# A trunk layer with RWKV-7 and attention heads on one core: interleaved output projection, substitution on blocks of 32, and a step of its own for the loads of the inverse's blocks

## The chip, the cores and the metric

The kernel runs on one core of one Trainium2 chip. The metric is the device time of one execution in microseconds, the median of the runs shown. Weights and activations lie in device memory ahead of the run, and all results are written back to it.

## What is computed

One layer over 1024 prompt frames (a new stream) and 64 sample frames (a continued stream) of width 1024, all in fp32. Cut to what matters:

```
mod = silu(c) @ w_ada + b_ada                  # 6 x 1024 per stream
sh1, sc1, gt1, sh2, sc2, gt2 = split(mod, 6)
h = rms_norm(x) * (1 + sc1) + sh1
proj = h @ w_in                                # 1024 -> 3336 columns
# RWKV-7, 8 heads of 64; per frame:
#   sa = S @ -kk ;  S = S * w + sa (kk * a)^T + v k^T ;  y = S @ r
# attention with forget gates, 8 heads of 64:
#   softmax(q k^T / 8 + decay bias, causal) @ v
mix = concat(y_rwkv, y_fox) @ w_out
x = x + gt1 * mix
h2 = rms_norm(x) * (1 + sc2) + sh2
ffn = (silu(h2 @ w_gate) * (h2 @ w_up)) @ w_down   # 2816 wide
y = x + gt2 * ffn
```

The final RWKV states, the last projected row, the attention keys, values and forget logs are outputs too.

## The kernel before

Activations lie with the features on the 128 partitions and the frames along them. The frames are worked in two halves: half 0 has 512 prompt frames, half 1 the other 512 and the 64 sample frames (576). An fp32 product is made of three fp32r products: each operand is split into a high part, made on ACT, and the rest, made on DVE or POOL, and PE adds hi x hi, lo x hi and hi x lo (`mm3`, L290 to 296; `split`, L209 to 216; the flag `pool_lo` chooses between POOL and DVE). A tile scheduler lays out each engine's list of instructions from the program's order and the data dependences; it also decides which of the ready instructions of two steps stands first. All transfers are issued on SP.

The stages in time:

* The modulation, 48 tiles of w_ada. A tile is loaded whole (512 KB), multiplied by the vector of both streams in eight small matmuls (`ada_mm`, L190), copied by ACT to a row, transposed on PE (L198), and reduced and biased on DVE (L200, L201). The first 16 come ahead of everything; the 32 others run as "background", one with each load of w_in.
* A phase for each half, in an order written out by hand (`ORDER`, L35 and L36). A letter is a step, its digit a pair of heads: Z projects r, k and v of a pair; D makes the decay; A the matrices of the chunks; B the chain over the chunks; N the group norm. Q, K, q, k, V project, norm and store the attention's operands, C copies the cache, L, O and S are small. The last pair's chain of a half, B3, is not in the string: it is done in the next stage, for half 0 as the step T3 of half 1's phase, for half 1 beside the attention's first heads.
* Attention of half 0 and of half 1, with the output projection of half 0 between the heads of half 1.
* `x1_sq` and `h2_make`: the second norm and the FFN's operands of half 0; then the output projection of half 1; then the same for half 1.
* The FFN, products of seven block combinations in place of eight (`ffn`, `fast_half`, `fast_prep`). Its unit is an item: w_gate or w_up of a pair of 128-column blocks, first for half 0, then for half 1. A weight item's combinations are made on DVE and ACT one item ahead. The gated result goes to device memory (actscr).
* The down projection: loads of actscr, their split, and PE's products in groups of four of the 22 blocks (`down`, L1244), the residual on DVE (L1248).

The RWKV step A and B need some detail, since most of the change is there. The frames of a half are cut into chunks of 64: 8 in half 0, 9 in half 1. Step A makes for each chunk and each of a pair's two heads the 64 x 64 lower triangle of the products of kk with k's multiples (pA on PE, L464, masked on DVE by `amask`, L466: tile At). The chain needs (I - triangle)^-1. It is found from the inside: the 16 x 16 blocks on the diagonal (four for each head and chunk, two of them a 32-block; 64 in half 0's A, 72 in half 1's, one on each partition) are written to device memory (dm) and read back as one block a partition (mb). They are inverted there by forward substitution on DVE: 15 steps of two instructions, a product into tb (L488) and a sum into wb (L490). The inverses and their transposes go to device memory again (dw, du), with zeros standing around them since the start.

Step B reads them back with eight transfers (gt and inv, 32-blocks), and merges them: 16-blocks to 32 by three sets of small 32 x 32 matmuls (all by the helper at L523: pg1 with a mask product on DVE at L530, pw1 with a sum at L535, pu1 with copies on ACT at L540), then 32-blocks to 64 by two more sets (pgt, pu12). Then it transposes kb and v, and runs the chain: for each chunk pR on PE (L597), a copy R on DVE and on ACT (one head each, L599, L600), pSA (L610), a copy sv on both (L611, L612), pS (L613), and the next state on DVE (L617), while POOL has made the decayed state sd (L604); pY (L608, L618) is the output. Nothing in a chain can run ahead; the matmuls of the projections (named pmm) stand between its matmuls on PE's list.

Of the kernel before, what the change touches and what calls it, by code (L numbers as in the profile page):

```python
# [16 lines left out]
P = 128  # L17
# [17 lines left out]
ORDER = ("Z0 D0 A0 L B0 D1 Z1 Q0 N0 A1 C0 Z2 q0 D2 V0 O A2 K0 k0 B1 K1 Z3 Q1 q1 V1 N1 D3 A3 V2 C1 S k1 Q2 Q3 B2 q2 N2 K2 k2 V3 K3 k3 C2 C3 q3",  # L35
         "T3 Z0 D0 A0 L Z1 K0 D1 U3 B0 A1 D2 Z2 Q0 N0 k0 A2 q0 D3 Q1 B1 K1 q1 Z3 A3 k1 V2 N1 V1 B2 V0 Q2 q2 K3 N2 Q3 q3 K2 k3 k2 V3")  # L36
# [28 lines left out]
class K:  # L65
# [7 lines left out]
    def consts(self):  # L73
# [14 lines left out]
        self.ct = self.cmid.tile([P, KT, 32], F32, name="ct")  # L88
# [23 lines left out]
    def consts2(self):  # L112
# [17 lines left out]
        for h in range(2):  # L130
            am = self.amask[:, h]
            nc.gpsimd.memset(am[64 * h:64 * h + 64, 0:64], -1.0)
            for r in (0, 64):
                nc.gpsimd.affine_select(out=am[r:r + 64, 0:64], in_=am[r:r + 64, 0:64], compare_op=ALU.is_gt,
                                        fill=0.0, base=0, pattern=[[1, 64]], channel_multiplier=-1)
                nc.gpsimd.affine_select(out=am[r:r + 64, 64:128], in_=am[r:r + 64, 64:128], compare_op=ALU.is_ge,
                                        fill=0.0, base=0, pattern=[[1, 64]], channel_multiplier=-1)
# [199 lines left out]
    def rwkv_persist(self):  # L337
# [4 lines left out]
        for t in self.inv:  # L342
# [3 lines left out]
        self.qmask = self.fper.tile([P, 32], F32, name="qmask")  # L346
        nc.vector.tensor_reduce(self.qmask[:, 0:1], self.ident.rearrange("p (q i s) -> p i q s", i=2, s=16)[:, 1],
                                axis=AX.XY, op=ALU.add)
        nc.vector.tensor_copy(self.qmask[:, 1:16], self.qmask[:, 0:1].to_broadcast([P, 15]))
        nc.gpsimd.memset(self.qmask[:, 16:32], 0.0)  # L350
        zero = self.inv[0].rearrange("p c t -> p (c t)")[0:72, 0:512]
        for t in self.dw + self.du:
            nc.sync.dma_start(t.rearrange("g x s t -> (g x s t)").rearrange("(p t) -> p t", p=72), zero)
# [63 lines left out]
    def rwkv_a(self, hf, j, z, d):  # L417
# [21 lines left out]
        nc.vector.tensor_tensor(rk[:, 0:nch, 0:64], ch(kk), pp[:, 0:nch, 0:64], op=ALU.mult)  # L439
# [30 lines left out]
        nb = 2 * ng  # L470
        dm = self.dpool.tile([2, ng, 2, 16, 16], F32, tag="dm", name="dm")
        for h in range(2):
            for x in range(2):
                for i in range(2):
                    o = 32 * x + 16 * i
                    nc.sync.dma_start(dm[i, h * nch:(h + 1) * nch, x].rearrange("g s t -> s g t"),
                                      At[64 * h + o:64 * h + o + 16, 0:nch, 0, h, o:o + 16])
        mb = self.rpool.tile([72, 16, 16], F32, tag="mb", name="mb")
        nc.sync.dma_start(mb[0:2 * nb], dm.rearrange("i g x s t -> (i g x) s t"))
        wb = self.rpool.tile([72, 16, 16], F32, tag="wb", name="wb")  # L480
        tb = self.rpool.tile([72, 64], F32, tag="tb", name="tb")
        nc.gpsimd.memset(wb[0:2 * nb], 0.0)
        nc.gpsimd.affine_select(out=wb[0:2 * nb], in_=wb[0:2 * nb], compare_op=ALU.not_equal, fill=1.0, base=0,
                                pattern=[[-1, 16], [1, 16]], channel_multiplier=0)
        for s in range(15):
            m = 15 - s
            t_ = tb[0:2 * nb, 0:m * (s + 1)].rearrange("p (a b) -> p a b", b=s + 1)
            nc.vector.tensor_tensor(t_, mb[0:2 * nb, s, s + 1:16].unsqueeze(2).to_broadcast([2 * nb, m, s + 1]),  # L488
                                    wb[0:2 * nb, s:s + 1, 0:s + 1].to_broadcast([2 * nb, m, s + 1]), op=ALU.mult)
            nc.vector.tensor_tensor(wb[0:2 * nb, s + 1:16, 0:s + 1], wb[0:2 * nb, s + 1:16, 0:s + 1], t_, op=ALU.add)  # L490
        nc.vector.tensor_copy(mb[0:2 * nb], wb[0:2 * nb].rearrange("p s t -> p t s"))

        dw, du = [t[j % 2] for t in (self.dw, self.du)]
        for i in range(2):
            r, o = slice(i * nb, (i + 1) * nb), slice(16 * i, 16 * i + 16)
            for d, t in ((dw, wb), (du, mb)):
                nc.sync.dma_start(d[0:ng].rearrange("g x s t -> (g x) s t")[:, o, o], t[r])
        return zv, rk, kb, pc, bon, At, dw, du

    def rwkv_b(self, hf, j, st):  # L500
# [6 lines left out]

        inv, gt = self.inv[j % 2], self.gt
        for h in range(2):
            g = slice(h * nch, (h + 1) * nch)  # L510
            for x in range(2):
                r = slice(64 * h + 32 * x, 64 * h + 32 * x + 32)
                nc.sync.dma_start(gt[r, 0:nch], dw[g, x].rearrange("g s t -> s g t"))
                nc.sync.dma_start(inv[r, 0:nch, r], du[g, x].rearrange("g s t -> s g t"))
# [10 lines left out]

        g1 = self.rpool.tile([P, 9, 32], F32, tag="g1", name="g1")
        pg = small("pg1", (0, 1), lambda h, c, r, o: (At[r, c, 0, h, o], gt[r, c]))
        for h in range(2):
            hs = slice(64 * h, 64 * h + 64)
            nc.vector.tensor_tensor(g1[hs, 0:nch], pg[h][hs, 0:nch],  # L530
# [1109 lines left out]
```

## Time and profile before

| | us |
|---|---|
| median of 3 runs | 1759.04 (1754.95 to 1759.44) |
| the profiled execution, its own time | 1761.91 |
| its span in the profile | 1760.2 |
| mean granted TensorE clock | 0.974 of full speed |
| phase of half 0 | about 44 to 400 |
| phase of half 1 | about 400 to 690 |
| chains B0 to B3 of half 0 | 150 to 181, 213 to 246, 300 to 328, 371 to 398 |
| chains of half 1 | 473 to 507, 550 to 584, 626 to 657, 696 to 731 |
| attention, first scores to last | 705.5 to 921 |
| output projection of half 1 | about 951 to 1014 |
| FFN | 1001 to 1490 |
| down projection | 1490 to 1757 |

The times in the profile count from the start of its span. A chain's times are those of its first and last pSA. PE is TensorE's matmuls, PEld its weight loads; an engine's busy time is the union of its instructions. The table was read from the timeline and from single tiles' rows.

### The profile page before, as it was taken

The page shows a single profiled execution, that of the slowest core. Times are in us where ns is not written, and L with a number is a line of the kernel's source. Part 1 is how long each engine was busy: PE and PEld are TensorE (multiplying, and loading weights), DVE is VectorE, ACT ScalarE, POOL GpSimd, SP SyncE. Part 2 cuts the span into 40 slices and gives each one's busy share as a digit, 9 for nine tenths or more (in the row PEclk, how much of TensorE's full clock was granted, in tenths as well). Part 3 has the DMA queues.
Part 4 walks back from the last instruction along what each step waited for, and adds up shares of the span by engine and source line. Part 5 has one row for each costly group of instructions (what it writes and reads, how often), then busy time and mean ns, then how long its engine had stood idle before and what let it go on. Part 6 is the DMA issues. An engine that isn't in the chain of part 4 may idle for free.

```text
span 1760.2 us, 33567 instructions
## 1 busy us (share of the span) xinstructions
PE 1673.6 (95%) x12893; PEld 1454.0 (83%) x12893; DVE 1105.8 (63%) x2518; ACT 728.0 (41%) x1532; POOL 267.6 (15%) x468
## 2 busy tenths in 40 slices
PE   5999999999999998889999779999999999999999
PEld 3676666688888886666888779999999999999998
DVE  6676676757786753777876685556666654444434
ACT  4435454543555344566776363233333222112110
POOL 2102121121222122100212300000000000222221
PEclk9999999999999997889999899999999999999999
DMA  8435356642233336376663302222222224533313
GB/s 314 151 87 157 116 165 195 184 122 71 76 75 92 107 84 167 96 203 166 158 188 128 106 34 83 74 74 74 74 74 78 79 89 134 182 99 93 99 36 120
DMA packets 136143, 207.10 MB, mean 118 GB/s; under 512 B 64687, under 2 KB 72911, under 8 KB 135983
## 3 DMA queue, kind: packets, MB, share of 16 engines
q1 hardware_dynamic: 135982, 204.95, 39.1%
q8 instruction: 102, 1.67, 0.4%
q14 instruction: 59, 0.48, 0.1%
HBM read 157.65 MB, written 47.25 MB: 116 GB/s over the span
## 4 chain that ended last, share of the span: by engine, by line
PE 81%; DVE 7%; ACT 6%; issue 3%; DMA 3%; POOL 1%; SPq 0%; ACTq 0%; DVEq 0%; POOLq 0%
PE pd L1244 15%; PE pfc L1143 7%; PE pfe L1143 7%; PE pfa L1143 7%; PE pmm L294 5%; PE pmm L296 5%; PE pmm L295 5%; PE pfb L1143 4%; PE pav L952 2%; PE pbs L375 2%; PE ppt L930 2%; PE pA L464 2%; PE pS L613 1%; PE po L295 1%; PE po L294 1%
## 5 line engine op out<-in xcount | busy, mean ns | idle before, releaser
L216 POOL TENSOR_TENSOR wlo<-wraw,whi 128x512 fp32r<-128x512 f32 (+2 forms) x64 | 107.1, 1675 | 777.5 <-ACT whi L212 772.2
L294 PE MATMUL pmm<-hhi,whi 128*128 128x288 f32 (+1 forms) x624 | 220.3, 353 | 1.0 <-ACT pb L317 0.7
L295 PE MATMUL pmm<-hlo,whi 128*128 128x288 f32 (+1 forms) x624 | 216.8, 347 | 1.4 <-DVE hlo L272 1.4
L296 PE MATMUL pmm<-hhi,wlo 128*128 128x288 f32 (+1 forms) x624 | 215.6, 345 | 0.0
L212 ACT CAST whi<-wraw 128x1024 fp32r<-128x1024 f32 (+2 forms) x116 | 99.2, 855 | 234.8 <-PE pd L1244 168.1
L1244 PE MATMUL pd<-ah,whi 128*128 128x512 f32 (+1 forms) x528 | 173.3, 329 | 2.2 <-ACT ah L212 2.2
L1244 PE MATMUL pd<-al,whi 128*128 128x512 f32 (+1 forms) x528 | 174.1, 330 | 0.5 <-DVE al L216 0.5
L1244 PE MATMUL pd<-ah,wlo 128*128 128x512 f32 (+1 forms) x528 | 173.7, 329 | 0.0
L1248 DVE SCALAR_TENSOR_TENSOR x1t<-pd,mod,x1t 128x512 f32<-128x512 f32 x192 | 90.6, 497 | 132.1 <-PE pd L1244 131.0
L294 PEld LDWEIGHTS pmm<-hhi,whi 128*128 128x128 f32 x624 | 119.2, 191 | 14.3 <-ACT pb L317 2.5
L295 PEld LDWEIGHTS pmm<-hlo,whi 128*128 128x128 f32 x624 | 119.4, 191 | 11.1 <-DVE hlo L272 2.1
L296 PEld LDWEIGHTS pmm<-hhi,wlo 128*128 128x128 f32 x624 | 119.4, 191 | 10.2 <-issue 1.2
L1143 PE MATMUL pfc<-hh,hS 128*128 128x256 f32 (+1 forms) x352 | 102.3, 291 | 8.0 <-ACT hh L1045 5.6
L1244 PEld LDWEIGHTS pd<-ah,whi 128*128 128x128 f32 x528 | 99.8, 189 | 10.5 <-ACT ah L212 2.7
L1244 PEld LDWEIGHTS pd<-al,whi 128*128 128x128 f32 x528 | 99.8, 189 | 8.5 <-DVE al L216 0.7
L1244 PEld LDWEIGHTS pd<-ah,wlo 128*128 128x128 f32 x528 | 99.9, 189 | 7.5
L604 POOL TENSOR_SCALAR sd<-sv,pc 64x64 f32<-64x64 f32 x136 | 72.1, 530 | 202.7 <-DVE sv L617 190.3
L1143 PE MATMUL pfc<-hl,hS 128*128 128x256 f32 (+1 forms) x352 | 102.4, 291 | 0.0
L1143 PE MATMUL pfc<-hh,lS 128*128 128x256 f32 (+1 forms) x352 | 102.2, 290 | 0.0
L1143 PE MATMUL pfa<-hh,whi 128*128 128x256 f32 (+1 forms) x352 | 102.0, 290 | 0.0
L1143 PE MATMUL pfa<-hl,whi 128*128 128x256 f32 (+1 forms) x352 | 101.8, 289 | 0.0
L1143 PE MATMUL pfa<-hh,wlo 128*128 128x256 f32 (+1 forms) x352 | 101.4, 288 | 0.0
(360 smaller groups left out, 4471.6 us busy)
## 6 DMA issues: line engine op xcount, KB each, us to landing
wraw<-in_w_in_dram SPq DMA_DIRECT2D x52, 512.0 KB
wada<-in_w_ada_dram SPq DMA_DIRECT2D x48, 512.0 KB
as<-actscr SPq DMA_DIRECT2D x22, 544.0 KB
wraw<-in_w_gate_dram SPq DMA_DIRECT2D x22, 512.0 KB
wraw<-in_w_up_dram SPq DMA_DIRECT2D x22, 512.0 KB
wraw<-in_w_down_dram SPq DMA_DIRECT2D x40, 256.0 KB
wraw<-in_w_out_dram SPq DMA_DIRECT2D x16, 512.0 KB
actscr<-sg SPq DMA_DIRECT2D x22, 288.0 KB
```

Source lines behind the costliest of these rows:

```text
L212: nc.scalar.copy(hi, src)
L216: eng.tensor_tensor(lo, src, hi.bitcast(F32), op=ALU.subtract)
L294: nc.tensor.matmul(ps[0:M, 0:n], whi[:, k, 0:M], xhi[:, k, off:off + n], start=(k == 0), stop=False)
L295: nc.tensor.matmul(ps[0:M, 0:n], whi[:, k, 0:M], xlo[:, k, off:off + n], start=False, stop=False)
L296: nc.tensor.matmul(ps[0:M, 0:n], wlo[:, k, 0:M], xhi[:, k, off:off + n], start=False, stop=(k == kt - 1))
L375: nc.tensor.matmul(ps[:, 0:n], w, x[:, off:off + n], start=True, stop=True)
L464: nc.tensor.matmul(pa[h][:, i], kb[hp, c + i], rk[hp, c + i], start=True, stop=True)
L604: nc.gpsimd.tensor_scalar(sd[hsl[h]], sv[hsl[h], c, h], pc[hsl[h], c], None, op0=ALU.mult)
L930: nc.tensor.transpose(pt[0:rows, b - b0, t * P:t * P + qn], p[0:qn, b * P:b * P + rows], self.ident[0:qn, 0:qn])
L1143: nc.tensor.matmul(ps, l[:, k], r[:, s, k], start=(first and k == 0 and y == 0), stop=(k == 3 and y == 2), skip_group_check=True)
L1244: nc.tensor.matmul(ps[:, 0:n], w[:, i], x[:, t:t + n], start=(i == 0 and y == 0), stop=(i == len(fs) - 1 and y == 2))
L1248: nc.vector.scalar_tensor_tensor(dst, ps[:, so - off:so - off + l], self.mod[:, 40 + o, b:b + 1], dst, op0=ALU.mult, op1=ALU.add)
```

## The change

**Substitution on blocks of 32.** The 16-blocks go, and with them the mask, the three merges and the zeros in dw and du. Step A writes 32 x 32 blocks, and half as many transfers carry them out. Each block is read back to two partitions (0 and up, 64 and up): one makes columns 0 to 15 of the inverse, the other 16 to 31. 31 steps of two instructions on 100 partitions replace 15 on 64 or 72. The columns of kk stand in even-odd order within each 32 (rk is written by two products, and the mask `amask` has the same pattern); a step s has then 2(16 - o)e elements a partition, with o = (s+1)//2 and e = s//2 + 1.

**Loads as a step.** The eight transfers of gt and inv become `rwkv_g`, a step G. The string holds only G3 (half 0: after k3 and ahead of C2 C3 q3; half 1: after q3 and ahead of K2). For every other pair they are issued at the start of B, as before. Besides, "K1 q1 Z3" of half 1 becomes "Z3 K1 q1".

**Interleaved output projection.** Half 0's operands for the FFN are made between the eight output projections of half 1 (`next(h2)`), not ahead of them. The first two tiles of w_out are loaded ahead. From there on all splits are on DVE and none on POOL: w_out's for half 1 and w_down's in the down projection. w_gate's first pair is loaded at o = 4 and prepared at o = 5.

**Modulation.** Tiles 40 to 47, which only the down projection's gate uses, leave the background: 40 to 43 run behind the output projection, 44 to 47 (`gap`) between the FFN's first products for half 0 and half 1's operands. w_up's first pair is loaded only behind them, and prepared in the first item of half 1.

**Activations.** The first two blocks of actscr are loaded ahead of the last FFN item (`early`), the next two at its start in half 1 (`mid`); they are split in its steps 1 to 4.

```diff
-        for s in range(15):
-            m = 15 - s
-            t_ = tb[0:2 * nb, 0:m * (s + 1)].rearrange("p (a b) -> p a b", b=s + 1)
-            nc.vector.tensor_tensor(t_, mb[0:2 * nb, s, s + 1:16].unsqueeze(2).to_broadcast([2 * nb, m, s + 1]),
-                                    wb[0:2 * nb, s:s + 1, 0:s + 1].to_broadcast([2 * nb, m, s + 1]), op=ALU.mult)
-            nc.vector.tensor_tensor(wb[0:2 * nb, s + 1:16, 0:s + 1], wb[0:2 * nb, s + 1:16, 0:s + 1], t_, op=ALU.add)
-        nc.vector.tensor_copy(mb[0:2 * nb], wb[0:2 * nb].rearrange("p s t -> p t s"))
+        for p in (0, 64):
+            nc.sync.dma_start(mb[p:p + nb], dm.rearrange("g x s t -> (g x) s t"))
...
+        m4 = mb.rearrange("p s (e t) -> p s e t", e=2)
+        w4 = wb.rearrange("p (e t) c -> p e t c", e=2)
+        for s in range(31):
+            o, e = (s + 1) // 2, s // 2 + 1
+            m, sh = 16 - o, [100, 2, 16 - o, e]
+            t_ = tb[:, 0:2 * m * e].rearrange("p (x a b) -> p x a b", x=2, b=e)
+            nc.vector.tensor_tensor(t_, m4[:, s, :, o:16].unsqueeze(3).to_broadcast(sh),
+                                    w4[:, s % 2, s // 2, 0:e].unsqueeze(1).unsqueeze(1).to_broadcast(sh), op=ALU.mult)
+            nc.vector.tensor_tensor(w4[:, :, o:16, 0:e], w4[:, :, o:16, 0:e], t_, op=ALU.add)
...
-        pg = small("pg1", (0, 1), lambda h, c, r, o: (At[r, c, 0, h, o], gt[r, c]))
...
-        pg = small("pw1", (0,), lambda h, c, r, o: (inv[r, c, r], g1[r, c]))
...
-        pg = small("pu1", (0, 1), lambda h, c, r, o: (g1[r, c], inv[r, c, r]))
...
+            elif op == "G":
+                self.rwkv_g(hf, j, st[j])
+                got.add(j)
             elif op == "B":
+                if j not in got:
+                    self.rwkv_g(hf, j, st[j])
...
-            self.background = [lambda t=t: self.ada_fin(self.ada_mm(t)) for t in range(16, 48)]
+            self.background = [lambda t=t: self.ada_fin(self.ada_mm(t)) for t in range(16, 40)]
...
+            self.pool_lo = False
...
-            for _ in self.h2_make(halves[0], self.x1_rs(halves[0], acc)):
-                pass
+            w1 = [self.load_w(A["w_out"][o], [P, KT, P]) for o in range(2)]
+            h2 = self.h2_make(halves[0], self.x1_rs(halves[0], acc))
...
             for o in range(KT):
-                self.outproj(halves[1], o, ("ab", "ce")[o % 2])
+                self.outproj(halves[1], o, ("ab", "ce")[o % 2], w1[o] if o < 2 else None)
                 acc = self.x1_sq(halves[1], o, acc)
+                next(h2, None)
...
+            def gap():
+                ada_run(ada[4:])
+                raw.append(self.fast_raw(pair("w_up")))
+            ada_run(ada)
...
+            def early():
+                h2s[2].close()
+                self.spool.pools["as"] = L(early_s, "sas0", 2)
+                for f in range(2):
+                    pre.append(self.act_load(f, None))
```

How this moves instructions, at three places. First PE's list where the chain B0 of half 0 begins, before (pmm is the projection of w_in, all else the chain):

```order
L597 MATMUL pR<-sv,At 128x128
L294 MATMUL pmm<-hhi,whi 128x512
L608 MATMUL pY<-rk,sv 128x128
L295 MATMUL pmm<-hlo,whi 128x512
L296 MATMUL pmm<-hhi,wlo 128x512
L610 MATMUL pSA<-R,inv_692 128x64
L294 MATMUL pmm<-hhi,whi 128x512
L295 MATMUL pmm<-hlo,whi 128x512
L296 MATMUL pmm<-hhi,wlo 128x512
L294 MATMUL pmm<-hhi,whi 128x512
L295 MATMUL pmm<-hlo,whi 128x512
L613 MATMUL pS<-sv,kb 128x128
```

and the same place after the change (the names with numbers are the same tiles, other copies):

```order
L547 MATMUL pu_1215<-inv_689,gt 32x32 x8
L573 MATMUL pvt<-ident,z 128x128 x4
L595 MATMUL pR<-sv,At 128x128
L606 MATMUL pY<-rk,sv 128x128
L608 MATMUL pSA<-R,inv_689 128x64
L611 MATMUL pS<-sv,kb 128x128
L616 MATMUL pY<-At,sv 128x128
L595 MATMUL pR<-sv,At 128x128
```

The projection's matmuls no longer stand between the matmuls of the first three chunks; they stand ahead of the chain. Second, DVE's list in the same chain, where the substitution of the next pair (A1) stands between the chain's copies R and sv, before:

```order
L488 TENSOR_TENSOR tb<-mb,wb 64x15
L331 TENSOR_SCALAR z<-pb,omu 128x512
L490 TENSOR_TENSOR wb<-wb,tb 64x15
L200 TENSOR_REDUCE mred<-pada 128x2
L488 TENSOR_TENSOR tb<-mb,wb 64x28
L332 SCALAR_TENSOR_TENSOR z<-pb,vc,z 128x512
L490 TENSOR_TENSOR wb<-wb,tb 64x14x2
L599 COPY R<-pR 64x64
L488 TENSOR_TENSOR tb<-mb,wb 64x39
L201 TENSOR_SCALAR mod<-mred,vc 128x2
L490 TENSOR_TENSOR wb<-wb,tb 64x13x3
```

and after:

```order
L494 TENSOR_TENSOR tb<-mb,wb 100x32
L597 COPY R<-pR 64x64
L496 TENSOR_TENSOR wb<-wb,tb 100x32
L494 TENSOR_TENSOR tb<-mb,wb 100x30
L496 TENSOR_TENSOR wb<-wb,tb 100x2x15
L609 TENSOR_SCALAR sv<-pSA 64x64
L494 TENSOR_TENSOR tb<-mb,wb 100x60
L496 TENSOR_TENSOR wb<-wb,tb 100x2x15x2
L494 TENSOR_TENSOR tb<-mb,wb 100x56
L615 SCALAR_TENSOR_TENSOR sv<-pS,pc,sd 64x64 x2
L496 TENSOR_TENSOR wb<-wb,tb 100x2x14x2
L494 TENSOR_TENSOR tb<-mb,wb 100x84
```

The steps are about twice as many, with larger arrays, and stand two to four between two copies of the chain. Third, PE's list in the FFN's first item, between the products of half 0 and of half 1 (pfe, pfb and the others are the seven products), before:

```order
L1143 MATMUL pfe<-hh_11725,hS_12268 128x256
L1143 MATMUL pfe<-hl_11726,hS_12268 128x256
L1143 MATMUL pfe<-hh_11725,lS_12269 128x256
L1143 MATMUL pfb<-hh_11725,hS_12264 128x256
L1143 MATMUL pfb<-hl_11726,hS_12264 128x256
```

and after:

```order
L1141 MATMUL pfe<-hh_11069,hS_11547 128x256
L1141 MATMUL pfe<-hl_11070,hS_11547 128x256
L1141 MATMUL pfe<-hh_11069,lS_11548 128x256
L190 MATMUL pada<-wada,ct 32x128 x16
L198 MATMUL pada<-ident,mrow 128x128 x2
L190 MATMUL pada<-wada,ct 32x128 x16
L198 MATMUL pada<-ident,mrow 128x128 x2
L1141 MATMUL pfb<-hh_11069,hS_11543 128x256
```

Four modulation tiles now stand between two products of one item.

More of the change, by code (lines that the diff above doesn't have):

```diff
@@ L344, in rwkv_persist @@
         self.gt = r.tile([P, 9, 32], F32, name="gt", tag="gt")
[L346 to L353, printed above, removed]
+        self.mb = r.tile([100, 32, 32], F32, name="mb", tag="mb")
+        nc.gpsimd.memset(self.mb, 0.0)
         self.pp = r.tile([P, 9, 65], F32, name="pp", tag="pp")
```

148 lines of the change are left out of this document (83 added, 65 removed).

## Prediction

> **What bounds the kernel now.** I read the page's head first, then a table by stage (windows of the span, each with the busy time of every engine, the granted clock, the DMA share), then the groups by line, and last the chain that ended last. Columns of the windows: stretch, its length, PE, PEld, DVE, ACT, POOL busy in us (instructions), PEclk, DMA share, GB/s.
>
> ```profile
> span 1760.2 us, 33567 instructions
> PE 1673.6 (95%) x12893; PEld 1454.0 (83%) x12893; DVE 1105.8 (63%) x2518; ACT 728.0 (41%) x1532; POOL 267.6 (15%) x468
> ```
> ```profile
> 44.00:400.00 356.00, 342.57 (x2859) 252.15 (x2858) 239.72 (x638) 170.57 (x369) 64.14 (x146) 0.97 0.50 145
> 400.00:690.00 290.00, 283.94 (x2792) 242.94 (x2790) 197.59 (x545) 137.74 (x326) 65.71 (x130) 0.99 0.34 91
> 950.00:1056.00 106.00, 84.00 (x587) 80.98 (x586) 82.63 (x120) 59.31 (x87) 22.00 (x6) 0.92 0.23 74
> 1056.00:1477.00 421.00, 420.98 (x3340) 420.74 (x3340) 247.19 (x474) 127.84 (x240) 1.66 (x1) 1.00 0.24 75
> 1477.00:1500.00 23.00, 20.25 (x130) 18.76 (x129) 12.46 (x19) 6.43 (x7) 1.82 (x1) 0.93 0.83 268
> 1500.00:1757.00 257.00, 256.92 (x1555) 234.29 (x1553) 113.76 (x207) 44.47 (x63) 57.86 (x46) 1.00 0.32 101
> ```
> The reader is to see five stages. In the FFN (1056 to 1477) and the down projection (1500 to 1757) PE has no gap: only fewer matmuls would shorten them, and the change takes none away there. In the two phases (44 to 400, 400 to 690) PE is busy 96% and 98% of the time, but its weight loads only 71% and 84%, where the FFN shows 420.74 of 421. Ends of matmuls are modelled, so a matmul that was issued early and waits for an operand counts as busy; the phases hold some waiting that the PE column hides. DVE has 67% and 68% there. Around the output projection of half 1 (950 to 1056) PE stands idle 22 us, and at the turn to the down projection 2.75 us.
>
> The Trainium skill, page "Perfetto Trace Analysis", section "Identifying the Most-Contended Engine", says that TensorE's matmul busy share is no good measure and that the share of its weight loads is. By the busy row all work taken off PE in the phases would be gained, which is rival R2 below; by the weight loads a good part is waiting on other engines, and the trace agrees so far as 71% against 100% in the FFN goes.
>
> **Part by part.** (a) PE work that leaves the phases: the three merges of 16-blocks to 32.
>
> ```profile
> L523 PE MATMUL pg<-gt,At 32*32 32x32 f32 x544 | 13.5, 193 | 0.0
> L523 PE MATMUL pu<-inv,g 32*32 32x32 f32 x544 | 12.9, 193 | 0.0
> L523 PE MATMUL pw<-g,inv 32*32 32x32 f32 x272 | 11.6, 195 | 0.5 <-DVE g L530 0.5
> 182.37 0.69 PE L523 MATMUL pg<-gt,At 32*32 32x32 f32 x32
> ```
> The groups sum to 38.0 us; 1360 matmuls at the timeline's 0.69 us per 32 are 29.3. I take 32. (b) Eight of the 48 modulation tiles leave the phases:
>
> ```profile
> L190 PE MATMUL pada<-wada,ct 128*32 128x128 f32 x768 | 37.0, 290 | 12.5 <-DMA wada<-in_w_ada_dram 10.8 <-DVE mod L201 1.0 <-DVE x L270 0.4
> L198 PE MATMUL pada<-ident,mrow 128*128 128x128 f32 x48 | 14.3, 298 | 4.0 <-ACT mrow L193 3.9
> ```
> (37.0 + 14.3) / 48 = 1.07 us a tile, 8.6 for eight. PE's list in the phases gets about 41 us shorter.
>
> (c) DVE. The substitution goes from 15 to 31 steps of two operations, and the arrays get larger. A step's price comes from its size:
>
> ```profile
> L490 DVE TENSOR_TENSOR wb<-wb,tb 64x15 f32<-64x15 f32 x8 | 1.4, 169 | 0.2
> L490 DVE TENSOR_TENSOR wb<-wb,tb 64x63 f32<-64x63 f32 x8 | 1.7, 212 | 0.1
> L488 DVE TENSOR_TENSOR tb<-mb,wb 64x15 f32<-64x15 f32 (+15 forms) x120 | 24.7, 206 | 3.3 <-DMA mb<-dm 1.2
> L490 DVE TENSOR_TENSOR wb<-wb,tb 64x15 f32<-64x15 f32 (+15 forms) x120 | 23.9, 199 | 2.7
> L530 DVE TENSOR_TENSOR g<-pg,qmask 64x256 f32<-64x256 f32 (+1 forms) x16 | 7.0, 436 | 5.2 <-PE pg L523 4.9
> L535 DVE TENSOR_TENSOR gt<-gt,pw 32x128 f32<-32x128 f32 (+1 forms) x16 | 4.6, 287 | 4.5 <-PE pw L523 4.3
> L491 DVE COPY mb<-wb 64x256 f32<-64x256 f32 (+1 forms) x8 | 3.4, 422 | 0.2
> L439 DVE TENSOR_TENSOR rk<-kk,pp 128x512 f32<-128x512 f32 (+1 forms) x8 | 5.8, 720 | 0.1
> L200 DVE TENSOR_REDUCE mred<-pada 128x2 f32<-128x8 f32 x48 | 7.6, 159 | 7.4 <-PE pada L198 7.2
> L201 DVE TENSOR_SCALAR mod<-mred,vc 128x2 f32<-128x2 f32 x48 | 11.3, 236 | 0.8
> ```
> From 15 to 63 elements a partition the step grows from 169 to 212 ns: 0.156 us + 0.0009 us an element. The new steps have 2(16 - o)e elements, 2992 over the 31; so an A step costs 2 x (31 x 0.156 + 2992 x 0.0009) = 15.0 us, and the eight 120, where they cost 24.7 + 23.9 = 48.6: 71 more. The merge's DVE operations go (7.0 + 4.6), and the eight tiles' share of mred and mod (8/48 of 18.9 = 3.2); the copy of twice the size (3.4 now) and rk's product in two pieces (5.8 now) add about 3, an estimate from their rows. Net about +60, which raises DVE from 67% to near 79% of a shorter phase. It is not shown what four strided dimensions cost: one third more or less on the 120 gives +20 to +100.
>
> How much lies on the path? The steps of A(j+1) stand in DVE's queue within the chain of B(j). A chunk of the chain is a round over PE, DVE and ACT; as long as projection matmuls stand between on PE, it is covered. Two chains, and DVE's old steps in the second:
>
> ```profile
> 300.00:328.00 28.00, 26.71 (x169) 19.37 (x169) 16.94 (x50) 12.42 (x31) 7.23 (x16) 1.00 0.64 179
> 473.00:507.00 34.00, 33.65 (x231) 29.13 (x230) 24.33 (x85) 15.49 (x40) 12.31 (x26) 1.00 0.19 42
> 473.00:507.00 34.00, 6.33 (x31) 0.00 (x0) 1.00 0.19 42
> ```
> The first (B2 of half 0) has no old steps in it and 28 - 16.94 = 11.1 us of DVE idle: 15.0 us of steps overflow by 4. The second (B0 of half 1) has 9.7 idle and about 2 x 6.33 of old steps that go: 22 us of room, so the steps fit. What is left there is the queue: three of the chain's DVE operations a chunk wait half a step, 0.12 us, 24 times: 2.9, of which the shorter old steps took about 1. So 2 each for the five chains with room, 10, and 4 for the one without. B0 of half 0 has something more: its first three chunks (15 chain matmuls) now run with no projection matmul between, only one modulation tile. Three chunks at 28/8 = 3.5 us, less 15 matmuls of some 0.2 us, are 7.5, say 8 us of bare PE. On the path: 8 + 4 + 10 = 22. Ends: 8 if all steps fit and only the bare chunks stay; 60 if all the net DVE work lands there. The phases: -41 + 22 = -19.
>
> (d) The end of half 1. Here the last chain runs beside the attention:
>
> ```profile
> 657.00:696.00 39.00, 34.43 (x399) 28.01 (x397) 13.96 (x30) 21.31 (x48) 8.64 (x13) 0.85 0.51 144
> 696.00:732.00 36.00, 31.37 (x147) 24.91 (x148) 19.24 (x69) 13.48 (x47) 7.95 (x22) 0.69 0.37 98
> ```
> After the change the score matmuls begin with six of the nine chunks behind them, not three; projection matmuls behind B2's chain are 42, not 103. Three chunks more without cover cost 3 x 36/9 = 12 at most; the loads of B3's blocks as a step G3 ahead of K2 (in half 0, ahead of C2, C3, q3) save the wait for eight DMAs ahead of the chain, and PE's idle in both windows, 4.57 + 4.63, could go with some of the 31% that the clock lacks. +12 and -14: I take 0. On SP, G3's eight issues now stand ahead of K2's and k3's transfers; the share of 0.51 leaves room for them. The dm transfers fall from 8 to 4 and mb's rise from 1 to 2, dw/du's from 4 to 6: hidden behind projection matmuls, since the order holds an A's chain back: B0's begins after 312 of them in half 0, where it was 270, and after 1263, where it was 1123, in half 1. If that cover failed, the 9 us that each A step takes longer would show ahead of B0, 9 in each half, which stays inside the 60.
>
> (e) Between output projection and FFN. The chain of waits there:
>
> ```profile
> 969.99 9.28 POOL wlo L216
> 1001.98 2.62 POOL wlo L216
> ```
> The split of w_out goes from POOL to DVE, the first two loads come earlier, and half 0's FFN operands are made between the projections instead of ahead of them. The 9.28 and 2.62 go (11.9); of the 22 us of PE idle the eight tiles' 8.6 may fill some. Against that, the split on DVE (eight of the kind below, and DVE is busy 78% of the window), two groups of modulation tiles whose DVE results (159 + 236 ns a tile) stand between the operands that the FFN waits for, and w_up's load, now issued after them, which may be late by some 3 to 4 us. I take -5, between -16 (idle less a quarter) and +5.
>
> ```profile
> L216 DVE TENSOR_TENSOR wlo<-wraw,whi 128x1024 fp32r<-128x1024 f32 x52 | 63.4, 1219 | 23.9 <-ACT whi L212 23.0 <-DMA dm<-At 0.6
> ```
> (f) The first gated activations are loaded before the last FFN items:
>
> ```profile
> 1479.99 5.29 DMA as<-actscr
> 1487.77 6.46 DMA as<-actscr
> ```
> The two DMAs on the chain are 11.75 us, but in that window PE lacks only 2.75 us and 7% of clock, 1.6: -4, between 0 and -11.7. (g) In the down projection the split goes to DVE, 40 of about 0.6 us (half of the 1219 above): 24 us more on 113.76 of 257. Hidden; if it were not, PE would wait 0.6 us at most at each of 8 outputs, 5.
>
> Sum: -19 + 0 - 5 - 4 = -28. The profiled execution took 1761.9 (span 1760.2 and 1.7 around it): 1734. The median of the runs shown, 1759.04, is 2.9 below it: 1731.
>
> **The rivals.** R2, PE really is the bound of the phases: the chains keep cover, all 41 are gained, the idle of the turn goes (-10 with the tiles filling it), and the DMA of the activations gives its 11.7: -63, 1696. For it: the busy column, and DVE's room of 22 us in five chains. Against: PEld at 71%, and the three bare chunks.
>
> R3, slower: DVE becomes the bound of the phases. All 71 us of added steps lie on the path since each stands in one queue with the chain's copies: -41 - 9 + 71 = +21, 1780. It decides from where more than 50 of the 71 are on PE's path. For it: the chain of window 300 to 328 lacks room already, and strided operands may cost more than the fit. Against: 22 us of room in the others.
>
> R4, slower: the steps and POOL's products exclude each other.
>
> ```profile
> L604 POOL TENSOR_SCALAR sd<-sv,pc x136: 435/443/1476, 74.2 to 727.5; 64x64 f32<-64x64 f32 x136
> L488 DVE TENSOR_TENSOR tb<-mb,wb x120: 139/200/630, 104.5 to 631.0; 64x15 f32<-64x15 f32 x8, 64x28 f32<-64x28 f32 x8, 64x39 f32<-64x39 f32 x8, 64x48 f32<-64x48 f32 x8
> ```
> Min, median, max: both have a tail (1476, 630 ns). If every sd blocked the steps, 16 x 0.443 = 7.1 us a chain over six chains are 43 us: -28 + 43 = +15, 1774; from 28 on it decides. Against: the medians lie at the minimum or close to it, though the old steps ran in chains too. The Trainium skill, page "SBUF — State Buffer", section "Who interferes with whom", states this exclusion for a DVE instruction with two SBUF inputs and a GpSimd one that reads SBUF. It speaks against 62 such steps a chain, and for the split's move to DVE; the medians show little of it in the chains, the tails allow it.
>
> R5, no change: the chains and the attention's start give back what PE gained (22 grows to 41, the turn gives nothing): 1759. That the change does not do what it says can only be for the loads: only G3 is a step of its own, the other six are called at B as before, and so add nothing.
>
> **How the numbers follow.** Forecast .57, R2 .24, R3 .07, R4 .05, R5 .07. Its terms' half-widths, 4.4 (PE), 12 (chains; what lies beyond is R3's), 10 (d), 10 (e), 5 (f), add as squares to 20: the forecast's own range is 1711 to 1751. The range for all, 1690 to 1760, takes in R2 nearly whole and half of R5, and leaves out R3 and R4. This kernel's runs can tell 0.3%, 5.3 us, from no change. Faster: .57 + .24 = .81; same .07; slower .12.
>
> **What would show it.** In the changed kernel: no pg, pu, pw in the groups; steps at 120 us in 496 instructions, at 0.24 us each (0.16 or 0.32 would move (c)); DVE near 79% in the phases; B0's chain of half 0 with PE at 75% for its first 10 us; the phases ended near 670 rather than 690; the window after them by 5 shorter; FFN and down unchanged at 421 and 257. PE's weight-load share above 80% in half 0 with the phase 40 shorter would mean R2, idle of PE on DVE's wb or tb in every chain R3, steps over 0.4 us beside sd R4. The forecast is wrong if the phases end within 8 us of 690 or before 655, or if a stage behind them moves by more than 16.

## The result and the profile after

The changed kernel takes 1788.26 us (median of 4 runs, 1787.15 to 1788.93) against 1759.11 before: ratio 1.0164, interval 1.0138 to 1.0190. It is 29 us slower. The forecast was 1731 and its range ended at 1760; of the rivals, R3 (DVE becomes the bound of the phases, 1780) came nearest, with a chance of .07.

The page's head and the windows of the changed kernel (columns as above):

```profile
span 1786.6 us, 30814 instructions
PE 1672.7 (94%) x11533; PEld 1453.1 (81%) x11533; DVE 1183.8 (66%) x2804; ACT 721.1 (40%) x1500; POOL 212.3 (12%) x432
```
```profile
44.00:400.00 356.00, 328.45 (x2071) 241.67 (x2070) 263.85 (x730) 164.39 (x340) 81.11 (x159) 0.92 0.46 138
400.00:690.00 290.00, 271.58 (x1925) 234.58 (x1924) 216.44 (x638) 124.56 (x288) 70.66 (x130) 0.94 0.29 81
```

1360 matmuls are gone and PE's busy time is what it was, 1672.7 for 1673.6. In the phases PE is busy less than before, its weight loads have fallen to 68% (half 0), and the granted clock has fallen from .97 and .99 to .92 and .94. PE got less to do and waits more. DVE went from 437 us in the phases (239.72 + 197.59) to 480, or 74% of them: on average there is room.

Where the time went is read from single tiles' rows: the last projection product, the first and last scores, and the down projection's first and last product (min/median/max ns, then first and last start). Before:

```profile
L296 PE MATMUL pmm<-hhi,wlo x624: 288/297/796, 34.9 to 679.1; 128*128 128x288 f32 x104, 128*128 128x512 f32 x52
L902 PE MATMUL psc<-k1x,qsx x104: 280/400/797, 705.5 to 921.0; 128*128 128x512 f32 x64, 128*128 128x256 f32 x32, 128*128 128x320 f32 x8
L296 PE MATMUL po<-mixfh,wlo x96: 289/296/598, 806.3 to 1010.5; 128*128 128x288 f32 x64, 128*128 128x512 f32 x32
L1244 PE MATMUL pd<-ah,whi x528: 292/296/502, 1489.9 to 1756.4; 128*128 128x288 f32 x89, 128*128 128x512 f32 x87
```
After:

```profile
L296 PE MATMUL pmm<-hhi,wlo x624: 289/298/797, 35.2 to 704.3; 128*128 128x288 f32 x104, 128*128 128x512 f32 x52
L900 PE MATMUL psc<-k1x,qsx x104: 281/396/774, 745.6 to 958.8; 128*128 128x512 f32 x64, 128*128 128x256 f32 x32, 128*128 128x320 f32 x8
L296 PE MATMUL po<-mixfh,wlo x96: 289/296/632, 840.4 to 1039.4; 128*128 128x288 f32 x64, 128*128 128x512 f32 x32
L1252 PE MATMUL pd<-ah,whi x528: 292/297/400, 1520.4 to 1782.5; 128*128 128x512 f32 x88, 128*128 128x288 f32 x88
```

| up to | later by | the stage's own share |
|---|---|---|
| last projection | 25.2 | +25.2 |
| first scores | 40.1 | +14.9 |
| last scores | 37.8 | -2.3 |
| last output projection | 28.9 | -8.9 |
| first down product | 30.5 | +1.6 |
| last down product | 26.1 | -4.4 |

All of the loss lies ahead of the attention's first scores. Behind them the change gives back what it was to give.

Now the steps. Groups of the changed kernel:

```profile
L494 DVE TENSOR_TENSOR tb<-mb,wb 100x120 f32<-100x120 f32 (+14 forms) x248 | 65.1, 262 | 4.0
L496 DVE TENSOR_TENSOR wb<-wb,tb 100x120 f32<-100x120 f32 (+14 forms) x248 | 63.6, 256 | 4.2 <-DVE sv L609 0.2
```

496 operations, 128.7 us; 120 were forecast. So the price of a step was right within 7%. What was wrong is where they stand. Half 1's step A0, DVE from 471 us on:

```profile
471.02 1.21 DVE L216 TENSOR_TENSOR wlo<-wraw,whi 128x1024 fp32r<-128x1024 f32 x1
472.16 0.29 DVE L494 TENSOR_TENSOR tb<-mb,wb 100x144 f32<-100x144 f32 x1
472.38 0.81 DVE L430 SCALAR_TENSOR_TENSOR kk<-z,kk,sq 128x576 f32<-128x576 f32 x1
473.11 0.29 DVE L496 TENSOR_TENSOR wb<-wb,tb 100x144 f32<-100x144 f32 x1
473.33 0.67 DVE L436 TENSOR_TENSOR rk<-kk,pp 128x288 f32<-128x288 f32 x1
473.83 0.28 DVE L494 TENSOR_TENSOR tb<-mb,wb 100x128 f32<-100x128 f32 x1
```

The first 17 of A0's 62 operations stand almost alone; from 462 us on each of them (0.16 to 0.30 us) is followed by another operation of 0.2 to 1.2 us, of the next pairs' preparation or a split, and the next step stands behind that. No gap is left between them. The 62 operations, 15.6 us of work, run from 458.0 to 496.6; before, A0's 30 ran from 435.4 to 446.2, in a queue that was nearly as full there (11.00 of 12 us). The same stretches of the two A0 (half 0: 98 to 141; half 1: 458 to 497) as windows of the changed kernel:

```profile
98.00:141.00 43.00, 42.24 (x252) 30.25 (x251) 38.41 (x116) 17.34 (x30) 3.02 (x10) 1.00 0.44 139
458.00:497.00 39.00, 32.66 (x204) 27.76 (x203) 38.12 (x112) 19.64 (x36) 3.11 (x10) 0.91 0.15 45
```

DVE is busy 38.12 of 39 us, and most pieces of the chain of waits in this stretch are DVE's. B0 of half 1 began at 520, where it began at 473. An engine with 26% of idle time over the phases is the bound just where a chain waits for it.

### The profile page after: what moved, and what is told of

The parts are those of the page before. It is cut to its first block, busy times and chain, and to the rows that moved or that the text cites. A ratio compares the mean times of both kernels' runs of the same rounds, so it can differ in the third digit from the quotient of the medians.

```text
span 1786.6 us, 30814 instructions
## 1 busy us (share of the span) xinstructions
PE 1672.7 (94%) x11533; PEld 1453.1 (81%) x11533; DVE 1183.8 (66%) x2804; ACT 721.1 (40%) x1500; POOL 212.3 (12%) x432
## 4 chain that ended last, share of the span: by engine, by line
PE 74%; DVE 11%; ACT 6%; DMA 4%; issue 3%; SPq 1%; POOL 0%; DVEq 0%; ACTq 0%; POOLq 0%
PE pd L1252 15%; PE pfc L1141 7%; PE pfe L1141 7%; PE pfa L1141 7%; PE pfb L1141 4%; PE pmm L294 4%; PE pmm L296 4%; PE pmm L295 3%; PE pav L950 2%; PE pA L461 2%; PE pbs L369 2%; PE ppt L928 2%; PE po L294 1%; PE po L296 1%; PE pS L611 1%
## 5 line engine op out<-in xcount | busy, mean ns | idle before, releaser
L295 PEld LDWEIGHTS pmm<-hlo,whi 128*128 128x128 f32 x624 | 123.1, 197 | 11.4 <-DVE hlo L272 1.9
L216 DVE TENSOR_TENSOR wlo<-wraw,whi 128x1024 fp32r<-128x1024 f32 (+2 forms) x108 | 103.7, 960 | 11.7 <-ACT whi L212 11.3
L602 POOL TENSOR_SCALAR sd<-sv,pc 64x64 f32<-64x64 f32 x136 | 82.1, 604 | 224.2 <-DVE sv L615 194.3
```

Source lines behind the costliest of these rows:

```text
L216: eng.tensor_tensor(lo, src, hi.bitcast(F32), op=ALU.subtract)
L295: nc.tensor.matmul(ps[0:M, 0:n], whi[:, k, 0:M], xlo[:, k, off:off + n], start=False, stop=False)
L602: nc.gpsimd.tensor_scalar(sd[hsl[h]], sv[hsl[h], c, h], pc[hsl[h], c], None, op0=ALU.mult)
```

## The experiments

Each kernel ran beside the kernel before on the same chip; "before" in a ratio is that. Executions of one kernel spread: the sixth run's twelve went from 1746.6 us, at a granted clock of .978, to 1765.0 at .969. So medians that differ by less than some 8 us are not taken apart here. The kernel before itself had medians from 1757.0 to 1760.8 in different groups of runs, so across groups the ratios are the better measure; where they say something else than the medians, both are given.

**Blocks of 16 again, the rest of the change** (the substitution, merges, transfers and masks of before in the changed kernel):

```diff
-        for s in range(31):
+        for s in range(15):
...
+        pg = small("pg1", (0, 1), lambda h, c, r, o: (At[r, c, 0, h, o], gt[r, c]))
```


> The changed kernel with the substitution on blocks of 16 and the three merges put back; all else of the change stays (order string, G3, modulation tiles, output projection, activations). Theory A, the 31 steps' DVE time is what costs: the phases end a little ahead of the kernel before (8.6 us of modulation tiles less), and the gains behind them stay (7.3 at the turn to the FFN, 4.4 at the turn to the down projection): about 1739, 1732 to 1748. Theory B, the cost is in the order and in the cover that the tiles and the moved steps gave: the phases stay late by 20 or more and PE has the merges again: 1770 to 1800.

1759.09, ratio 1.0009 (0.9991 to 1.0026). With the rest of the change in place, the whole 29 us hang on the substitution; but the rest by itself gains nothing either. Neither theory had that.

**The substitution on 32 alone** (the reverse, in the kernel before):

```diff
-        for s in range(15):
+        for s in range(31):
...
-        pg = small("pg1", (0, 1), lambda h, c, r, o: (At[r, c, 0, h, o], gt[r, c]))
```


> The kernel before with nothing but the substitution on blocks of 32 (loads of the inverse at B, order string, tiles and all later stages as before). Theory A: the phases lose what they lost in the changed kernel, 25 to 40 us, and nothing is gained behind them: 1785 to 1800. Theory B: PE's 32 us less are gained in part: 1725 to 1755.

1773.93, ratio 1.0094 (1.0070 to 1.0118): +15, between the two. Alone it is slower, but by half of the 29.

**No steps**, and **no steps in A0**, and later **no steps in A1 to A3**, all in the changed kernel. The identity stands in the place of the inverses that are left out, so these kernels do not compute the layer:

```diff
-        for s in range(31):
+        for s in range(0):
```
```diff
-        for s in range(31):
+        for s in range(31 if j else 0):
```
```diff
-        for s in range(31):
+        for s in range(0 if j else 31):
```


> The changed kernel without the 31 steps (the block's inverse is left out; the identity goes on in its place), with all transfers, the copy and everything else. Theory A: the whole cost of the steps goes, 126 us of DVE, and what is left is the gain of PE's shorter list: 1700 to 1725. Theory B: little changes, 1770 to 1790, since order and cover stay.

1728.46, ratio 0.9825 (0.9803 to 0.9847): the steps cost 60 us of the 1788. Theory A's size was nearly right (its range ended at 1725); the remaining gain over before is 31 us, with both the 38 us of merges on PE and 49 us of old steps on DVE gone.

> The changed kernel without the 31 steps in step A0 of both halves alone (two of eight substitutions left out). Theory A in the form that the two substitutions ahead of B0, where DVE is busy 38.1 of 39 us, cost most: half or more of some 66 us comes back, 1750 to 1765. Theory A in the form that all eight cost alike: 2/8 of 66, about 1772. Theory B: 1783 to 1790.

1758.29: 30 of the 60 us hang on two of the eight substitutions, 15 each on average. That is about the 15.6 us which the steps of one A0 take on DVE.

> The changed kernel without the 31 steps in A1, A2 and A3 of both halves (six of eight left out); A0 keeps them, the counterpart of the fourth run, where leaving out A0's two gave 30 of 60. If the places add up: 1788 - 30 = 1758, 1752 to 1764. If an A0 that is late is caught up when the later chains are free: 1740 or less. If the later ones cost all once A0 is late: 1728 to 1735.

1749.08, ratio 0.9938 (0.9919 to 0.9957): 39 us for six, 6.5 each. 30 + 39 is a little over 60: the places add up nearly, and A0's are worth more than twice a later one's. Not all of this is time in the phases. The last projection and the first scores, at 704.3 and 745.6 in the changed kernel, in one execution each without A0's steps, without the later ones, and without any:

```profile
L296 PE MATMUL pmm<-hhi,wlo x624: 289/296/855, 35.7 to 680.6; 128*128 128x288 f32 x104, 128*128 128x512 f32 x52
L900 PE MATMUL psc<-k1x,qsx x104: 281/397/774, 721.9 to 937.1; 128*128 128x512 f32 x64, 128*128 128x256 f32 x32, 128*128 128x320 f32 x8
```
```profile
L296 PE MATMUL pmm<-hhi,wlo x624: 289/297/799, 35.7 to 678.9; 128*128 128x288 f32 x104, 128*128 128x512 f32 x52
L900 PE MATMUL psc<-k1x,qsx x104: 280/396/797, 702.7 to 915.7; 128*128 128x512 f32 x64, 128*128 128x256 f32 x32, 128*128 128x320 f32 x8
```
```profile
L296 PE MATMUL pmm<-hhi,wlo x624: 289/297/797, 36.5 to 662.0; 128*128 128x288 f32 x104, 128*128 128x512 f32 x52
L900 PE MATMUL psc<-k1x,qsx x104: 281/397/793, 684.9 to 899.4; 128*128 128x512 f32 x64, 128*128 128x256 f32 x32, 128*128 128x320 f32 x8
```

Without A0's steps both come 24 us earlier. Without the later ones the projection ends 25 us earlier and the scores begin 43 earlier; without any it is 42 and 61. So in the phases an A0's steps cost some 12 us and a later pair's some 4, and 18 of the 60 us come back only at the start of the scores. They begin 41 us behind the last projection where the later steps stand, and 23 to 24 behind it where they do not (more on that under the order string).

**DVE made lighter, the steps kept.** The low part of w_in is left out of both kernels (50 splits of 1.22 us on DVE):

```diff
-            whi, wlo = self.load_w(self.A["w_in"][col // P], [P, KT, P])
+            raw = self.raw_w(self.A["w_in"][col // P], [P, KT, P])
+            whi = self.ring.tile([P, KT, P], F32R, tag="whi", name="whi")
+            self.nc.scalar.copy(whi, raw)
+            wlo = self.wz.unsqueeze(2).to_broadcast([P, KT, P])
```


> The changed kernel without the low part of w_in (zeros stand in its place as the weights of the third product; PE's list is the same): 50 splits of 1.22 us, 61 us, leave DVE in the phases, and the 31 steps stay. Theory A, DVE's queue is the bound where the steps stand: 129 us of steps cost 60, so 61 us less are worth some 28: 1745 to 1768. Theory E, it is the length of the row of 62 dependent steps and transfers ahead of each chain, whatever else DVE does: 1778 to 1788.

1763.17: 25 us less than the changed kernel, with all 31 steps in place. Half 1's A0 in this kernel runs from 440 to 476:

```profile
440.00:476.00 36.00, 34.22 (x238) 31.03 (x238) 34.19 (x106) 15.43 (x29) 2.03 (x9) 1.00 0.21 71
```

DVE is still busy 95% of it and the row is hardly shorter (36 us for 38.6), but it begins 18 us earlier, PE's clock is full there, and B0 begins at 499, not 520.

> The kernel before without the low part of w_in, the control of the ninth run: DVE had room there (67%), so by theory A little is gained, 1748 to 1759. If it gains as much as the changed kernel, 25 to 30, the ninth run says nothing on the steps.

1772.28, ratio 1.0071 (1.0046 to 1.0095): the same relief makes the kernel before slower by 13, which was not expected. It is no gain that both kernels share, so the 25 us speak for theory A. Why it is slower is open; its last projection ends at 694.7 for 679.4, so the loss lies in the phases. That the lists came out worse is a guess. It is a warning for all these runs: an edit can cost this much beside what it was made for.

**A product moved from DVE to ACT**, nothing left out:

```diff
-            nc.vector.tensor_scalar(z[:, o:o + l], pb[:, 1 + b + o:1 + b + o + l], om, None, op0=ALU.mult)
+            nc.scalar.activation(z[:, o:o + l], pb[:, 1 + b + o:1 + b + o + l], AF.Copy, scale=om)
```


> The changed kernel with the first product of each z (42 of 0.4 us, 16 us) on ACT and not on DVE; nothing is left out. Theory A, at 0.47 us per us of DVE: -7, 1778 to 1783. Theory E: 1785 to 1791. If ACT's queue then holds up the chains, 1795 or more.

1776.53, 12 us less than the changed kernel for 16 us of DVE; theory A had 7.

> The sixth run's kernel (blocks of 16, order string and tiles of before; the output projection interleaved, splits on DVE, early loads), with the first product of each z on ACT. By theory A DVE has room in this kernel's phases and the 16 us less give little: 1748 to 1756, against 1755 of the sixth run. If DVE's queue holds up chains here too, 1740 to 1747; if ACT's does, 1758 or more.

1763.68 against the sixth run's 1754.95 (below): 9 us more by the medians, 7 by the ratios (1.0028, 1.0010 to 1.0047, against 0.9988, 0.9965 to 1.0011). The expectation's main case, a small gain or none, ended at 1756. The kernel with short steps gains nothing by the edit; that the edit costs time there is at the edge of what is told apart here.

**The order string** (the strings of before in the first experiment's kernel and in the changed one), then the strings of after in the second's:

```diff
-K3 k3 G3 C2 C3 q3
+K3 k3 C2 C3 q3
...
-B1 Z3 K1 q1 A3
+B1 K1 q1 Z3 A3
...
-q3 G3 K2 k3 k2 V3
+q3 K2 k3 k2 V3
```


> The first experiment's kernel (blocks of 16, the rest of the change) with the order string of before too, so with the loads of G3 at B and Z3 behind K1 q1. That kernel stood at 1759, 12 to 20 us above what the gains behind the phases and the shorter PE list would give. Theory C, the order string costs this: 1745 to 1750. Theory D, the modulation tiles do, since in the phases they were cover for the chains (no gain there) and at the turn they stand in the way: 1756 to 1762.

1763.90 (ratio 1.0050, 1.0032 to 1.0068) against 1759.09: with blocks of 16 the string of before is no faster. Theory C is out there, and theory D's range (to 1762) was missed by 2.

> The changed kernel with the order string of before, so without G3 and with Z3 behind K1 q1; the substitution on 32 and all else stay. Theory C: the last chain begins earlier, 1770 to 1780. Theory D, or the steps alone: 1785 to 1790. A step G3 that does help would show as slower: 1791 to 1800.

1779.49 against 1788.26: with blocks of 32 it is 9 us faster by the medians, 6 by the ratios (1.0129, 1.0107 to 1.0152), whose intervals overlap, so the sign is likely and not shown.

> The second run's kernel (before with the substitution on 32) with the changed order string as well (G3, and Z3 ahead of K1 q1). That one stood at 1774, the changed kernel at 1788. Theory F, the string costs some 9 us once the steps are long: 1779 to 1788. Theory G, the string is harmless and the 14 us lie in the other parts: 1769 to 1778.

1795.61, ratio 1.0204 (1.0174 to 1.0234), against 1773.93 without the string: +22, or 19 by the ratios. That is the sign of theory F, the string costs with the long steps and not with the short ones, at more than twice its size (1788 was its end). Why it costs more here than in the changed kernel is open. Its two parts:

```diff
+K3 k3 G3 C2 C3 q3
...
+q3 G3 K2 k3 k2 V3
```


> The second run's kernel with the step G3 in both halves' strings, Z3 left where it was. The string as a whole cost 21 us there. If the loads as a step are what costs (in the thirteenth run's trace the first scores come 22 us after the last chain's start, against 0 to 10 with the string of before): 1786 to 1797. If Z3's place is: 1770 to 1778.

```diff
+B1 Z3 K1 q1 A3
```


> The second run's kernel with Z3 ahead of K1 q1 in half 1, without G3: the counterpart of the sixteenth. If the loads as a step cost the 21 us: 1770 to 1778; if Z3's place does: 1786 to 1797; halves: 1780 to 1786 in both.

1791.43 with G3 alone (ratio 1.0172, 1.0149 to 1.0195), 1783.34 with Z3 alone (1.0131, 1.0114 to 1.0147): +17 and +9 on 1773.93, 14 and 6 by the ratios. G3 costs clear of the spread; Z3's interval just meets the second run's. What G3 moves can be seen. The scores' rows of the second run (without G3; the traced execution, 1765.27, is the fastest of its four) and of the sixteenth (with it):

```profile
L895 PE MATMUL psc<-k1x,qsx x104: 281/396/774, 715.9 to 928.4; 128*128 128x512 f32 x64, 128*128 128x256 f32 x32, 128*128 128x320 f32 x8
```
```profile
L901 PE MATMUL psc<-k1x,qsx x104: 281/400/793, 738.3 to 953.7; 128*128 128x512 f32 x64, 128*128 128x256 f32 x32, 128*128 128x320 f32 x8
```

The last chain begins at 716.5 in both. Without G3 the scores begin with it, with G3 they begin 21.8 us later, when five of its nine chunks are done. The stretch of the bare chain in the sixteenth run:

```profile
717.00:738.00 21.00, 15.11 (x49) 11.47 (x50) 7.34 (x29) 2.29 (x10) 4.94 (x14) 0.50 0.66 181
```

49 matmuls in 21 us at half the clock: PE has nothing but the chain. A likely reading is that the scheduler, with the chain's blocks loaded early, takes it for ready and lists it ahead of the scores. The same five chunks stand ahead of the scores in the changed kernel; in the seventh, fourteenth and seventeenth run, without G3, there are three. But G3 alone does not do it. From the last projection to the first scores it is 41 us in the changed kernel and in the thirteenth and sixteenth run, which have both G3 and the long steps. It is 26 to 29 without G3 (before, second, seventh, fourteenth and seventeenth run), and 23 to 24 with G3 where the later pairs have short steps or none (first, third and eleventh run). So it takes both, which fits that the string costs nothing with blocks of 16; why it takes both is open.

**The tiles back in the background**, in the changed kernel, and there with the string of before as well:

```diff
-            self.background = [lambda t=t: self.ada_fin(self.ada_mm(t)) for t in range(16, 40)]
+            self.background = [lambda t=t: self.ada_fin(self.ada_mm(t)) for t in range(16, 48)]
```


> The changed kernel with all 32 modulation tiles in the background of the phases again. Theory D: the 8.6 us of PE work are cover there and the turn is rid of them, 1772 to 1782. If PE's work in the phases counts, as the prediction had it: 1788 to 1797.

1788.42: no change to be measured.

> The changed kernel with the order string of before and all 32 modulation tiles in the background: beside the second run's kernel it has only the interleaved output projection and what follows. Theory F: the string was the difference, 1768 to 1776 (the stages behind give up to 6 against the second run's 1774). Theory G: 1780 to 1790.

1771.26, ratio 1.0058 (1.0034 to 1.0082), 8 less than the seventh run's 1779.49. By the ratios it is 12, and the intervals do not meet. So the tiles' move gives nothing in one kernel and costs 8 to 12 in the other; nowhere did it gain 8.6.

**The late stages alone** (blocks of 16, string and tiles of before):

> As the fifth experiment, and all 32 modulation tiles in the background again as before: of the change there stay the interleaved output projection, the split on DVE behind it and the early loads of activations. Theories C and D both: the phases are those of before, 7.3 + 4.4 us are gained behind them: 1745 to 1751. If the turn's gain came from what the late phases had let pile up, it is not there without them: 1756 to 1761.

1754.95, ratio 0.9988 (0.9965 to 1.0011). A gain of 11.7 us would be 0.9933 and is excluded. In this kernel's trace the way from the last scores to the last down product is 1746.6 - 925.5 = 821.1 us, where it was 1756.4 - 921.0 = 835.4, so the gain is there in one execution; but its scores end 4.5 us later, and the executions spread. How much of it lasts is open. Beside the fifth run's kernel (1763.90), which differs from this one by the tiles' move alone, it is 9 us faster, and the intervals do not meet: the move costs there too. That is part of why the rest of the change gained nothing in the first experiment. No version that does all of the layer's work is faster than the kernel before beyond its interval.

## Why the prediction was wrong

* **Reading the bound.** That PE's busy column hides waiting in the phases was right, and R2 (1696) did not come, not even without any step (1728).
* **(a), (b), PE's 41 us.** Too much. With no steps at all, the gain is 31 us, and that with 49 us of old DVE steps gone too. The move of the eight tiles, forecast to take 8.6 off the phases, gained nothing beside e8; it cost 8 to 12 between e14 and e7, and 9 between e6 and e5. That they filled time in the phases in which PE waited fits this; it was not shown.
* **(c), the price of the steps.** Right: 128.7 us for 120.
* **(c), how much lies on the path: the step that failed.** The prediction compared 15.0 us of steps with the idle time of DVE in windows of the old kernel's chains, took 22 us on the path, and said that A0's longer row is hidden behind projection matmuls, at most 9 us a half. The runs showed 60 us for all the steps, 30 of them at the two A0, 15 each. For the substitution alone the prediction's terms give -32 + 22 = -10 us; e2 measured +15. The steps do not fill the idle time of a window: in half 1's A0 most of them stand one by one between other operations in a full queue, each of which delays the next. One reading under this step was wrong as well: the row of 6.33 us (x31) holds both operations of each of the 15 old steps and the copy, so it is not to be doubled. The room in that window was 9.7 + 6.3 = 16 us, not 22, for 15 us of steps, and the argument against R3 rested on the 22. The bound 60 for "all the net DVE work on the path" was in the text, as an end that the range left out, and R3 was that rival. R3 was to decide from 50 of the 71 added us on. How many of the 71 lay on the path is not known: the 60 us are for all 129 us of steps, and the 49 us of old steps had a price that was not measured. The substitution alone gave +15 (e2), and the order string on top of it brought the kernel past R3's 1780.
* **(c), the chains.** 2 to 4 us a chain were forecast for the increase. The six later substitutions cost 6.5 each for all of their steps: some 4 of it in the phases, which is not far off, the rest at the start of the scores. The sign named for the three bare chunks of B0 came (PE busy 7.91 of the 10 us from 159 on, at half the clock); their price of 8 us was not tried.
* **(d), the end of half 1.** Taken as 0 between -14 and +12. The first scores lose 15 on the last projection, 13 remain at the last scores. The sign of G3 was wrong: it was to save a wait, and with it five bare chunks stand ahead of the scores; e16 has it at +17 alone (14 by the ratios). This is the second term that failed.
* **(e), (f), (g).** Right in the changed kernel's trace: -8.9 + 1.6 for -5, -4.4 for -4, and no wait of the down projection on its splits. POOL's 9.28 and 2.62 us are gone from the chain of waits.
* **R4.** The median of sd stayed at 443 ns; its tail grew:

```profile
L602 POOL TENSOR_SCALAR sd<-sv,pc x136: 435/443/3400, 64.8 to 754.8; 64x64 f32<-64x64 f32 x136
```

From 72.1 us in all to 82.1: 10 us of POOL, where the rival needed 43 on the path.

Put together: +15 the substitution alone, +22 the string on top of it, -7 the rest (16, 19 and -7 by the ratios), which is the 29 measured. Each has some 5 us of doubt, and in another order the parts have other sizes, since the string costs nothing without the long steps.

## What to carry to other kernels

Work moved from a busy engine to one with idle time is priced where the receiving engine is waited for, not by its average: look at its share in the stretch ahead of each chain that waits, and at how many foreign operations stand between the dependent ones in its list. A long row of short dependent operations in an in-order queue takes the time of what stands between them too. And a step that is to make a long chain ready earlier can end with the chain listed earlier, ahead of independent work that would have covered it: look at the list that the scheduler makes, not only at the wait that is saved.

## What the runs showed of the hardware

A DVE operation with two inputs in SBUF took as long as the POOL operation that ran beside it. In the changed kernel, POOL:

```profile
685.88 2.47 POOL L216 TENSOR_TENSOR wlo<-wraw,whi 128x1024 fp32r<-128x1024 f32 x1 [1.38 <-ACT whi L212]
```
and DVE beside it:

```profile
685.89 0.26 DVE L496 TENSOR_TENSOR wb<-wb,tb 100x96 f32<-100x96 f32 x1
686.18 2.29 DVE L494 TENSOR_TENSOR tb<-mb,wb 100x104 f32<-100x104 f32 x1
688.40 0.27 DVE L615 SCALAR_TENSOR_TENSOR sv<-pS,pc,sd 64x64 f32<-64x64 f32 x1
```

A step of some 0.27 us took 2.29 and ended 0.1 us behind POOL's split. That POOL held it is inferred from these times. Of the 496 steps no other took over 0.6 us. The Trainium skill, page "SBUF — State Buffer", section "Who interferes with whom", says that such a DVE instruction contends with a GpSimd instruction that reads SBUF; this row agrees. The held step is on the chain of waits.

The granted clock can halve where the records show PE without a gap. The changed kernel at the start of half 1:

```profile
440.00:445.00 5.00, 5.00 (x22) 4.50 (x23) 0.96 (x3) 0.00 (x0) 0.00 (x0) 0.50 0.00 0
```

22 matmuls in 5 us at .50, and PE "busy" all the time: the busy column says nothing here, the count and the clock do. Over the span the mean clock fell from .974 to .953. Whether the lower clock is only a consequence of PE's waits or costs time of its own was not tried.
